# TensorE keeps the planned order in the attention, its first operands load beside the mLSTM, and a quarter of its branch projection becomes filler

## The chip, the cores and the metric

One core of a Trainium2 chip runs the whole kernel. The metric is the device time of one execution in microseconds (us). The core's engines work side by side, each through its own list of instructions in order: TensorE (PE, matmuls; its weight loads are PEld), VectorE (DVE), ScalarE (ACT), GpSimd (POOL) and SyncE (SP, which issues most of the DMA transfers; ACT issues some). They wait for each other by semaphores.

## What is computed

One step of a hybrid encoder layer on 1024 prompt rows and 8 x 16 sample rows, 1152 columns in all, as the kernel keeps tokens along the free axis:

```python
def merge_out(x, h_m, mz, h_a, az, gm, ga, w_bm, w_ba, w_out):
    u_m = jnp.einsum("btc,cd->btd", h_m * jax.nn.silu(mz), w_bm)
    u_a = jnp.einsum("btc,cd->btd", h_a * jax.nn.silu(az), w_ba)
    mix = jax.nn.sigmoid(gm) * u_m + jax.nn.sigmoid(ga) * u_a
    return x + jnp.einsum("btd,de->bte", mix, w_out)
```

Ahead of it stand a norm, one input projection (`w_in`) whose columns are q, k, v and gates of two branches, the mLSTM branch (4 heads of 128, chunkwise, gives `h_m`) and the attention branch (8 heads of 64, each chunk of 64 rows sees itself and 8 chunks before; samples see a cache; gives `h_a`). All is float32; a matmul of two float32 operands is made of three, on high and low halves: hi x hi, hi x lo, lo x hi.

## The kernel before, in words

All names are those of the code below; Lnnn is a line of it.

Stages, by the trace of before: 0 to 122 us input and first projections; 122 to about 410 products of the input projection (`pX`, `pW`, `pZ`); 410 to about 590 the mLSTM; 590 to 930 the attention; 930 to about 984 the branch projection of the attention (`wba`, 8 feature tiles j of 128 rows); then the output projection (`wout`, 8 tiles e).

A feature tile is `load_nt` (L588: weights from memory, split in halves `wh` on ACT and `wl` on DVE or POOL), then chunks of columns, each 3 matmuls for each of 8 (or 4) blocks of 128 rows into a PSUM tile `pm`, then an evacuation. The 16 merge-gate tiles (`gates`) and the 4 z tiles go in chunks of 288 columns (HC); the matmuls are `h_hi,wh`, `h_lo,wh`, `h_hi,wl` (L126 to L128). `g_evac` (L605) writes tanh into `tg`, which is stored to `tg_sc`, from a tag of two buffers. Eight gate tiles are filler in the mLSTM, the rest and the z tiles in the attention.

The attention runs in `run_line`: 32 tiles, four pairs p of heads times eight i of 128 rows. `attend` makes for each of two heads the scores `pS` (L940, L941), a softmax (maximum with bias on DVE, exp on ACT, reciprocal on DVE, scaling on POOL: `prob`), transposes `pT` in groups of up to five (L842), splits `PT` (ACT and DVE), then `pv` (L974). A pair needs `load_q` (two halves), `load_kv` and `load_bias`. The raw operands come through three `raw` buffers on SP and are split by ACT, DVE and POOL. The tile's result goes through `pvs`, `ot` and the store to `o_sc`, and is read again by `load_ops` (L1112) as operands `h2` of the branch projection.

What sets the order: `run_line` is a planner with a clock of its own, `line.now`. It emits the attention's steps when their planned times have come, two tiles alive at a time, and a filler step otherwise: gate and z chunks (`tile_work`), then the 32 chunks of `um_work` (the mLSTM's branch projection, 12 matmuls each, `tm` evacuation with the gate product, stored to `sm_sc`). Thirty filler steps stand ahead of the first. That is the order of the program; the framework's scheduler then orders every engine's instructions, TensorE's among them, by its own rules.

The branch projection: for each j a buffer `sa` (2 buffers) takes `sm_sc[j]` and `tg_sc[8+j]` by two DMAs of 0.59 MB (L1194, L1195). Three chunks of 384 columns (CH) each: DVE makes (tg + 1) * ps (L1199), POOL adds sm (L1200), ACT and DVE split into `x_hi`, `x_lo`. PSUM has six `pm` buffers here, and the output projection reads `x` of all eight j.

Of the kernel before, what the change touches and what calls it, by code (L numbers as in the profile page):

```python
# [6 lines left out]
F32 = mybir.dt.float32  # L7
# [7 lines left out]
P = 128  # L15
# [17 lines left out]
def emit(tc, a, o, ctx):  # L33
# [35 lines left out]
    sm_sc = dram.tile([8, P, T], F32, name="sm_sc")  # L69
    tg_sc = dram.tile([16, P, T], F32, name="tg_sc")  # L70
# [534 lines left out]
    def g_evac(j):  # L605

        def ev(c, ps):
            t_ = stg.tile([P, HC], F32, tag="th", name="tg")
            act.activation(out=t_, in_=ps, func=AF.Tanh, scale=0.5, bias=bh[:, 20 + j:21 + j])  # L609
            store(tg_sc[j], c, t_)  # L610
        return ev

    def z_evac(p):

        def ev(c, ps):
            z_ = stg.tile([P, HC], F32, tag="zs", name="zs")
            t_ = stg.tile([P, HC], F32, tag="th", name="th")
# [9 lines left out]

    esPS, pp = open_pool("pM", bufs=1, space=PSUM)
    esM1, m1 = open_pool("mlstm1", bufs=2, side="right")
    stg = m1  # L630
# [178 lines left out]
    esWp.close()  # L809
    turns = {t_: [wpA] for t_ in turns}  # L810
    stg = keep("stage", bufs=2, side="left")
# [35 lines left out]
    def parts_of(src, half):  # L847

        raw = spl.tile([P, 512], F32, tag="raw", name="raw", bufs=3)
        for x in range(2):  # L850
            sp.dma_start(raw[64 * x:64 * x + 64, :], src[:, half * 512:half * 512 + 512])
        return raw

    def load_q(p, half):
        for j in range(2):
            raw = parts_of(qk_sc[p][64 * j:64 * j + 64], half)
            Qh[p, j, half] = bp_.tile([P, 512], F32R, tag=f"qh{j}{half}", name="q_hi", bufs=1)
            Ql[p, j, half] = bp_.tile([P, 512], F32R, tag=f"ql{j}{half}", name="q_lo", bufs=1)
            split(Qh[p, j, half], Ql[p, j, half], raw, pool)

    def load_kv(p):

        for half in range(2):
            for j in range(2):
                raw = parts_of(qk_sc[4 + p][64 * j:64 * j + 64], half)
                if not half:
                    Kst[p, j] = bp_.tile([P, TP], F32R, tag=f"K{j}", name="Kst", bufs=2)
                k_ = Kst[p, j][:, half * 512:half * 512 + 512]
                act.activation(out=k_, in_=raw, func=AF.Copy)
                dve.tensor_tensor(out=k_[64:128], in0=raw[64:128], in1=f(k_[64:128]), op=ALU.subtract)  # L870
            if not half:
                Vst[p] = bp_.tile([P, NPT, 2, P], F32R, tag="Vst", name="Vst", bufs=2)
            vr = spl.tile([P, 512], F32, tag="raw", name="vraw", bufs=3)
# [47 lines left out]
    def attend(p, i):  # L921
# [59 lines left out]
        zt = ap_.tile([P, P], F32, tag="zt", name="zt", bufs=4)  # L981
# [22 lines left out]
    def sample(p):  # L1004
# [69 lines left out]
        zt = ap_.tile([P, P], F32, tag="zt", name="zt", bufs=4)  # L1074
# [35 lines left out]
    def load_ops(src, k0, order):  # L1110
        for kk, c in order:
            s = slice(c * HC, (c + 1) * HC)  # L1112
            raw = spl.tile([P, 512], F32, tag="raw", name="oraw", bufs=3)[:, 0:HC]
            sp.dma_start(raw, src[kk][:, s])
            split(*hcols(k0 + kk, c * HC, (c + 1) * HC), raw)

    def um_evac(j):

        def ev(c, ps):
            s = slice(c * HC, (c + 1) * HC)  # L1120
            t_ = stg.tile([P, HC], F32, tag="wqr", name="tm", bufs=4)
# [3 lines left out]
        return ev  # L1125

    def run_line():
# [7 lines left out]
        ums = um_work()  # L1135
        work = {"tiles": tile_work()}
        for _ in range(30):
            next(work["tiles"], None)
        line.now += 12000
        while True:  # L1140
# [26 lines left out]
            if not did and not work and ums is not None:  # L1167
# [4 lines left out]
                did = True  # L1172
            if not did:
                if not live and not samples and not work and ums is None:
# [9 lines left out]
    esH.close()  # L1184

# [5 lines left out]
    for j in range(8):  # L1191
        sa = fp.tile([P, 2 * T], F32, tag="sa", name="sa")
        sm, ta = sa[:, 0:T], sa[:, T:2 * T]
        sp.dma_start(sm, sm_sc[j])  # L1194
        sp.dma_start(ta, tg_sc[8 + j])  # L1195

        def ev_a(c, ps):
            s = slice(c * CH, (c + 1) * CH)
            dve.scalar_tensor_tensor(out=ta[:, s], in0=ta[:, s], scalar=1.0, in1=ps, op0=ALU.add, op1=ALU.mult)  # L1199
            pool.tensor_tensor(out=sm[:, s], in0=sm[:, s], in1=ta[:, s], op=ALU.add)  # L1200
            split(x_hi[:, j, s], x_lo[:, j, s], sm[:, s])

        feature_tile(load_nt(a["wba"][j], 4), lambda k, c: hcols(4 + k, c * CH, (c + 1) * CH), ev_a, 4, pp, "pu")
# [5 lines left out]
    for e in range(8):  # L1209
        def ev(c, ps):  # L1210
            xr = stg.tile([P, CH], F32, tag="wqr", name="xr", bufs=4).rearrange("p (i t) -> p i t", i=3)
# [116 lines left out]
```

## Time and profile before

| | us |
|---|---|
| runs | 1092.45, 1094.26, 1095.02 |
| median | 1094.26 |
| profiled execution, its own time | 1090.15 |
| its span | 1088.4 |
| TensorE busy in it | 1039.2 (95%) |
| VectorE, ScalarE, GpSimd busy | 641.5, 527.3, 409.6 |
| TensorE's mean granted clock | 0.991 of full speed |

The profile is of one execution. A window row gives the busy time of each engine in one stretch and, as "PEclk", the granted clock there (1.00 is 2.4 GHz, 0.50 is 1.2 GHz). A wait row tells on which engine and line an engine waited, and for what. A chain row is one piece of the work that ended last: its start, its length and what it was; a DMA in it is counted from issue to landing. Busy time of matmuls includes a modelled drain, so that a lone matmul shows some 0.3 us.

### The profile page before, as it was taken

Reading aid. Unit: us, or ns where it says so; the run is one execution under the profiler, and the core shown is the slowest. Engines: PE = TensorE matmul, PEld = TensorE weight load, DVE = VectorE, ACT = ScalarE, POOL = GpSimd, SP = SyncE. Lnnn points to the kernel's source line nnn. Section 1 sums busy time; section 2 is a strip of 40 time slices with the busy share of each in tenths; the row PEclk is TensorE's granted clock in tenths of the full one; section 3 lists DMA queues with packets and bytes.
Section 4 is the critical chain, followed back from the end, with each engine's and each line's share of the span. In section 5 each row is a group of like instructions: output and inputs, shape, how many; then the busy total and the mean of one; then the engine's idle time right before and its main releaser. Section 6 shows DMA issues by size and latency. Waiting matters only on the chain.

```text
span 1088.4 us, 22458 instructions
## 1 busy us (share of the span) xinstructions
PE 1039.2 (95%) x8090; PEld 1004.9 (92%) x8090; DVE 641.5 (59%) x1561; ACT 527.3 (48%) x1153; POOL 409.6 (38%) x517
## 2 busy tenths in 40 slices
PE   6999999999998999899999999999998998998998
PEld 6999999999998999898999889889898887998998
DVE  6944337585666546799975465354466657574221
ACT  7632147667577554544333566456565535322110
POOL 1132235344353334543334465355454433452000
PEclk8999999999999999899999999999999999999999
DMA  7554332332322228544547675564666874464332
GB/s 240 147 196 149 120 104 84 105 117 95 119 83 81 66 80 285 199 135 163 158 131 251 201 252 178 174 204 130 197 194 196 259 217 140 150 229 144 131 124 72
DMA packets 142516, 171.36 MB, mean 157 GB/s; under 512 B 27900, under 2 KB 106820, under 8 KB 141892
## 3 DMA queue, kind: packets, MB, share of 16 engines
q1 hardware_dynamic: 134196, 159.96, 46.2%
q10 hardware_dynamic: 8208, 9.97, 2.6%
q8 instruction: 64, 1.05, 0.4%
q14 instruction: 48, 0.39, 0.1%
HBM read 118.73 MB, written 51.13 MB: 156 GB/s over the span
## 4 chain that ended last, share of the span: by engine, by line
PE 61%; DMA 16%; DVE 11%; ACT 4%; issue 4%; POOL 2%; SPq 2%; ACTq 0%; DVEq 0%; POOLq 0%
PE pZ L471 10%; PE pm L127 10%; PE pm L126 10%; PE pm L128 10%; PE pW L471 7%; PE pX L471 7%; DMA raw<-qk_sc 3%; DMA sa<-tg_sc 2%; PE pT L842 2%; PE pv L974 2%; DMA oraw<-o_sc 1%; DMA sm_sc<-tm 1%; DMA oraw<-hm_sc 1%; DVE dx L741 1%; DVE kT L658 1%
## 5 line engine op out<-in xcount | busy, mean ns | idle before, releaser
L126 PE MATMUL pm<-h_hi,wh 128*128 128x288 f32 (+1 forms) x864 | 266.0, 308 | 9.4 <-ACT tg L609 6.6
L127 PE MATMUL pm<-h_lo,wh 128*128 128x288 f32 (+1 forms) x864 | 264.9, 307 | 1.1 <-DMA h_lo<-h_sc 1.1
L128 PE MATMUL pm<-h_hi,wl 128*128 128x288 f32 (+1 forms) x864 | 264.3, 306 | 0.0
L122 ACT ACTIVATE wh<-wr 128x512 fp32r<-128x512 f32 (+1 forms) x172 | 107.3, 628 | 151.9 <-PE pm L127 79.0
L126 PEld LDWEIGHTS pm<-h_hi,wh 128*128 128x128 f32 x864 | 164.9, 191 | 13.8 <-ACT tg L609 7.0
L127 PEld LDWEIGHTS pm<-h_lo,wh 128*128 128x128 f32 x864 | 165.1, 191 | 6.5 <-issue 4.2
L128 PEld LDWEIGHTS pm<-h_hi,wl 128*128 128x128 f32 x864 | 164.9, 191 | 1.7 <-issue 0.8
L123 DVE TENSOR_TENSOR wl<-wr,wh 128x512 fp32r<-128x512 f32 (+1 forms) x112 | 82.7, 742 | 40.7 <-ACT wh L122 37.6
L123 POOL TENSOR_TENSOR wl<-wr,wh 128x512 fp32r<-128x512 f32 x60 | 78.7, 1317 | 64.7 <-ACT wh L122 63.9
L450 POOL TENSOR_TENSOR wr<-wr 128x512 f32<-128x512 f32 x48 | 62.6, 1315 | 82.0 <-DVE wl L123 47.3
L833 POOL TENSOR_SCALAR prob<-prob,mx 128x640 f32<-128x640 f32 (+4 forms) x72 | 51.0, 709 | 88.0 <-DVE mx L832 69.4
L126 PE MATMUL pm<-wh,h_hi 128*128 128x256 f32 (+1 forms) x256 | 72.6, 287 | 2.6 <-DVE G L256 2.5
L831 ACT ACTIVATE prob<-prob,mx 128x640 f32<-128x640 f32 (+4 forms) x72 | 51.0, 708 | 47.4 <-DVE mx L830 45.8
L127 PE MATMUL pm<-wl,h_hi 128*128 128x256 f32 (+1 forms) x256 | 72.5, 286 | 0.0
L128 PE MATMUL pm<-wh,h_lo 128*128 128x256 f32 (+1 forms) x256 | 72.0, 284 | 0.0
L126 PE MATMUL pm<-x_hi,wh 128*128 128x384 f32 x192 | 64.8, 338 | 2.6 <-ACT x_hi L122 2.6
L474 DVE TENSOR_TENSOR ring<-pZ,ring 128x288 f32<-128x288 f32 x72 | 32.7, 455 | 58.5 <-PE pZ L471 52.7
L127 PE MATMUL pm<-x_lo,wh 128*128 128x384 f32 x192 | 64.8, 337 | 0.4 <-DVE x_lo L123 0.4
L128 PE MATMUL pm<-x_hi,wl 128*128 128x384 f32 x192 | 64.8, 337 | 0.0
L471 PE MATMUL pW<-S_hi,wh 128*128 128x288 f32 x192 | 56.8, 296 | 0.8 <-ACT ring L483 0.8
L471 PE MATMUL pZ<-S_hi,wh 128*128 128x288 f32 x192 | 56.7, 295 | 0.8 <-DVE ring L474 0.8
L471 PE MATMUL pX<-h_hi,wh 128*128 128x288 f32 x192 | 56.7, 295 | 0.5 <-ACT ring L481 0.5
(278 smaller groups left out, 2830.1 us busy)
## 6 DMA issues: line engine op xcount, KB each, us to landing
wr<-in_wn SPq DMA_DIRECT2D x88, 256.0 KB, 2.7
raw<-qk_sc SPq DMA_DIRECT2D x64, 128.0 KB, 2.8
kr<-in_Kc SPq DMA_DIRECT2D x16, 512.0 KB, 5.7
vr<-in_Vc SPq DMA_DIRECT2D x16, 512.0 KB, 3.2
xt<-in_x SPq DMA_DIRECT2D x9, 512.0 KB
v_sc<-vt SPq DMA_DIRECT2D x72, 64.0 KB, 1.7
u<-u_sc SPq DMA_DIRECT2D x8, 576.0 KB, 4.5
tg_sc<-tg SPq DMA_DIRECT2D x32, 144.0 KB, 2.1
```

What stands on the lines that cost most here:

```text
L122: act.activation(out=hi, in_=raw, func=AF.Copy)
L123: eng.tensor_tensor(out=lo, in0=raw, in1=f(hi), op=ALU.subtract)
L126: mm(ps, lhs[0], rhs[0], start=first, stop=False)
L127: mm(ps, lhs[0], rhs[1], start=False, stop=False)
L128: mm(ps, lhs[1], rhs[0], start=False, stop=last)
L450: pool.tensor_tensor(out=out[:, 0:512], in0=x[:, 0:512], in1=y[:, 0:512], op=ALU.subtract)
L471: mm(ps, w[l][:, k, :], x[r][:, k, :], start=first and k + l + r == 0, stop=k == KH - 1 and l == 1, skip_group_check=True)
L474: eng.tensor_tensor(out=out, in0=x, in1=y, op=ALU.add)
L831: act.activation(out=pt[:, :nk], in_=pt[:, :nk], func=AF.Exp, bias=mx[:, 1:2], accum_out=mx[:, 2:3])
L833: pool.tensor_scalar(out=pt[:, :nk], in0=pt[:, :nk], scalar1=mx[:, 3:4], scalar2=1.0, op0=ALU.mult, op1=ALU.mult)
L842: pe.transpose(pT[:, (n - n0) * P:(n - n0 + 1) * P], pt[:, n * P:(n + 1) * P], ident)
L974: mm(pv[:, j * 256:(j + 1) * 256], Vst[p][:, i + 1 - nb + n, j, :], st[:, n].rearrange("p a q -> p (a q)"), start=n == 0, stop=n == nb - 1)
```

## The change

Four things, and what follows from them in the pools.

1. `run_line()` stands in `tc.manual_schedule(engines={pe.engine})`: TensorE keeps the program's order in the attention, that is the planner's. The other engines stay with the scheduler. The head start grows from 30 to 64 filler steps and from 12000 to 24000 in `line.now`.
2. Pool `attnQ` is opened before the mLSTM. It holds the raw buffers, the first halves of q, and K and V of the even pairs; those of the odd pairs stay in `attnP`. So the loads of the first pair can be issued in the mLSTM, and on SP they stand among the heads' loads there; the first bias load stands on SP ahead of the cache loads `kr` and `vr` and not behind them. To make room, a weight pool is closed before the mLSTM (half as many `wh` and `wl` there), pool `stage` opens before the mLSTM, the gate tanh gets a tag of its own with five buffers, z one `th`, `zt` three, `tm` three.
3. `ua_work` is a new last filler: chunk 0 (288 of 1152 columns) of all eight `wba` tiles, 12 matmuls each, with sm and tg loaded by chunk, and the sum stored to a new scratch `xm_sc`. It may start once three tiles of each pair are done. Each `wba` weight is loaded once more for it.
4. The branch projection goes over pairs of j, in chunks of 288: chunks 1 and 2 of both, then chunk 3 of both, then the split of chunk 0 of both, which comes from `xm_sc`. An `sa` has three DMAs (864 columns of sm, 864 of tg, 288 of the sum).

```diff
-            t_ = stg.tile([P, HC], F32, tag="th", name="tg")
+            t_ = stg.tile([P, HC], F32, tag="tg", name="tg", bufs=5)
...
+    esWp.close()
+    turns = {t_: [wpA] for t_ in turns}
+    stg = keep("stage", bufs=4, side="left")
+    esQ, bq_ = open_pool("attnQ", bufs=1, side="left")
...
-        raw = spl.tile([P, 512], F32, tag="raw", name="raw", bufs=3)
+        raw = bq_.tile([P, 512], F32, tag="raw", name="raw", bufs=3)
...
-                    Kst[p, j] = bp_.tile([P, TP], F32R, tag=f"K{j}", name="Kst", bufs=2)
+                    Kst[p, j] = (bp_ if p % 2 else bq_).tile([P, TP], F32R, tag=f"K{j}", name="Kst", bufs=1)
...
-            t_ = stg.tile([P, HC], F32, tag="wqr", name="tm", bufs=4)
+            t_ = spl.tile([P, HC], F32, tag="wqr", name="tm", bufs=3)
...
+    def ua_evac(j):
+        def ev(c, ps):
+            s = slice(c * HC, (c + 1) * HC)
+            t_, m_ = (q_.tile([P, HC], F32, tag=q, name=q, bufs=3 if q == "wqr" else 2) for q_, q in ((spl, "wqr"), (stg, "zs")))
+            sp.dma_start(t_, tg_sc[8 + j][:, s])
+            sp.dma_start(m_, sm_sc[j][:, s])
+            dve.scalar_tensor_tensor(out=t_, in0=t_, scalar=1.0, in1=ps, op0=ALU.add, op1=ALU.mult)
+            pool.tensor_tensor(out=m_, in0=m_, in1=t_, op=ALU.add)
+            act.dma_start(xm_sc[j], m_)
+        return ev
+    def ua_work():
+        while any((p, i) not in done for p in range(4) for i in range(3)):
+            yield False
+        load_ops(o_sc, 4, [(kk, 0) for kk in range(4)])
+        for j in range(8):
+            w = load_nt(a["wba"][j], 4, eng=pool)
+            yield from chunk(0, w, lambda k, c: h_rhs(4 + k, c), ua_evac(j), 4)
...
-        for _ in range(30):
+        for _ in range(64):
-        line.now += 12000
+        line.now += 24000
...
-    run_line()
-    load_ops(o_sc, 4, [(kk, c) for kk in range(4) for c in range(4)])
+    with tc.manual_schedule(engines={pe.engine}):
+        run_line()
+    load_ops(o_sc, 4, [(kk, c) for c in range(1, 4) for kk in range(4)])
...
+    for j0 in range(0, 8, 2):
+        sas, ws = [], []
+        for j in (j0, j0 + 1):
+            sa = fp.tile([P, 2 * T], F32, tag="sa", name="sa")
+            sas.append((sa[:, 0:T], sa[:, T:2 * T]))
+            for t_, src in zip(sas[-1], (sm_sc[j], tg_sc[8 + j])):
+                sp.dma_start(t_[:, HC:], src[:, HC:])
+            sp.dma_start(sa[:, 0:HC], xm_sc[j])
+            ws.append(load_nt(a["wba"][j], 4))
...
+        for cs in ((1, 2), (3,)):
+            for j in (j0, j0 + 1):
+                for c in cs:
+                    feature_chunk(c, ws[j % 2], lambda k, c: h_rhs(4 + k, c), ev_a(j), 4, pp, "pu", HC)
+        for j in (j0, j0 + 1):
+            split(x_hi[:, j, 0:HC], x_lo[:, j, 0:HC], sas[j % 2][0][:, 0:HC])
```

TensorE in the middle of the attention (last pair), before: `pm` rows are fillers, `x3` stands for three in a row.

```order
L126 MATMUL pm<-h_hi,wh 128x288
L127 MATMUL pm<-h_lo,wh 128x288
L128 MATMUL pm<-h_hi,wl 128x288
L974 MATMUL pv<-PT,Vst 128x256 x3
L842 MATMUL pT<-ident,prob 128x128 x3
L940 MATMUL pS<-Kst,q_hi 128x320
L941 MATMUL pS<-Kst,q_lo 128x320
L940 MATMUL pS<-Kst,q_hi 128x320
L941 MATMUL pS<-Kst,q_lo 128x320
L974 MATMUL pv<-PT,Vst 128x256 x2
L842 MATMUL pT<-ident,prob 128x128 x2
L126 MATMUL pm<-h_hi,wh 128x288
```
And now, around the same kind of step:

```order
L127 MATMUL pm<-h_hi,wh 128x288
L128 MATMUL pm<-h_lo,wh 128x288
L129 MATMUL pm<-h_hi,wl 128x288
L976 MATMUL pv<-PT,Vst 128x256 x5
L844 MATMUL pT<-ident,prob 128x128 x5
L942 MATMUL pS<-Kst,q_hi 128x320
L943 MATMUL pS<-Kst,q_lo 128x320
L942 MATMUL pS<-Kst,q_hi 128x320
L943 MATMUL pS<-Kst,q_lo 128x320
L127 MATMUL pm<-h_hi,wh 128x288
L128 MATMUL pm<-h_lo,wh 128x288
L129 MATMUL pm<-h_hi,wl 128x288
```
The groups of `pv`, `pT` and `pS` are whole now, with twelve filler matmuls ahead of the `pv` and 36 behind the `pS`; before they were split in twos and threes.

TensorE where the attention ends and the branch projection begins (`pm` of 384 columns), before:

```order
L842 MATMUL pT<-ident,prob 128x128 x3
L974 MATMUL pv<-PT,Vst 128x256 x3
L842 MATMUL pT<-ident,prob 128x128 x2
L974 MATMUL pv<-PT,Vst 128x256 x5
L842 MATMUL pT<-ident,prob 128x128 x3
L974 MATMUL pv<-PT,Vst 128x256 x2
L842 MATMUL pT<-ident,prob 128x128 x5
L974 MATMUL pv<-PT,Vst 128x256 x3
L842 MATMUL pT<-ident,prob 128x128 x2
L974 MATMUL pv<-PT,Vst 128x256 x7
L126 MATMUL pm<-h_hi,wh 128x384
```
And now (the `pm` of 288 columns ahead of the last `pv` are fillers of `ua_work`, those behind it the branch projection):

```order
L127 MATMUL pm<-h_hi,wh 128x288
L128 MATMUL pm<-h_lo,wh 128x288
L129 MATMUL pm<-h_hi,wl 128x288
L976 MATMUL pv<-PT,Vst 128x256 x5
L844 MATMUL pT<-ident,prob 128x128 x5
L127 MATMUL pm<-h_hi,wh 128x288
L128 MATMUL pm<-h_lo,wh 128x288
L129 MATMUL pm<-h_hi,wl 128x288
L844 MATMUL pT<-ident,prob 128x128 x5
L976 MATMUL pv<-PT,Vst 128x256 x10
L127 MATMUL pm<-h_hi,wh 128x288
```
The end had no filler before; now filler stands up to the last two softmaxes, three matmuls lie between their transposes, and the last two groups of `pv` come together.

VectorE in the branch projection, its second and third j before (`sa<-sa,pm` is the product with the gate, `x_lo` the split that frees a buffer, `wl` a weight's low half):

```order
L123 TENSOR_TENSOR x_lo<-sa,x_hi 128x384 x3
L1199 SCALAR_TENSOR_TENSOR sa<-sa,pm 128x384 x3
L123 TENSOR_TENSOR wl<-wr,wh 128x512
L123 TENSOR_TENSOR x_lo<-sa,x_hi 128x384 x2
L1199 SCALAR_TENSOR_TENSOR sa<-sa,pm 128x384
L123 TENSOR_TENSOR x_lo<-sa,x_hi 128x384
L1199 SCALAR_TENSOR_TENSOR sa<-sa,pm 128x384
L123 TENSOR_TENSOR x_lo<-sa,x_hi 128x384
```
And its second pair now:

```order
L1242 SCALAR_TENSOR_TENSOR sa<-sa,pm 128x288 x3
L124 TENSOR_TENSOR wl<-wr,wh 128x512
L124 TENSOR_TENSOR x_lo<-sa,x_hi 128x288 x2
L124 TENSOR_TENSOR wl<-wr,wh 128x512
L124 TENSOR_TENSOR x_lo<-sa,x_hi 128x288
L1242 SCALAR_TENSOR_TENSOR sa<-sa,pm 128x288 x3
L124 TENSOR_TENSOR x_lo<-sa,x_hi 128x288 x5
```
Before, products and splits of one j follow each other; now three products of one j, its three splits, three of the other, and then five splits, of which the first is the one of chunk 0 of the first j.

## Rows read from the trace of the kernel before

**Rows 1.** TensorE and the others by stage; busy us (instructions), granted clock, DMA share, GB/s

```profile
410.00:590.00 180.00, 170.63 (x1318) 164.81 (x1317) 148.00 (x397) 76.27 (x168) 70.63 (x115) 0.98 0.56 182
590.00:910.00 320.00, 304.03 (x2769) 282.13 (x2769) 175.04 (x517) 179.19 (x418) 157.42 (x226) 0.99 0.65 202
910.00:930.00 20.00, 15.84 (x110) 13.66 (x110) 14.81 (x42) 11.96 (x28) 9.32 (x15) 1.00 0.33 99
930.00:984.00 54.00, 53.99 (x309) 53.51 (x308) 34.89 (x51) 16.14 (x31) 26.43 (x24) 1.00 0.60 213
984.00:1088.40 104.40, 97.88 (x556) 97.14 (x555) 26.69 (x44) 9.69 (x16) 3.41 (x3) 1.00 0.34 111
```

**Rows 2.** TensorE's waits, whole span; us in total, times, longest us

```profile
PE pm L126 <- ACT tg L609: 6.6, 2, 5.3
PE pS L940 <- DVE mx L828: 5.9, 6, 1.8
...
PE pm L126 <- ACT x_hi L122: 2.6, 1, 2.6
...
PE pT L842 <- POOL prob L833: 2.4, 4, 1.2
```

**Rows 3.** TensorE in three stretches of the mLSTM; busy us (instructions), clock, DMA share, GB/s

```profile
434.00:440.20 6.20, 1.45 (x11) 0.96 1.06 370
440.20:447.00 6.80, 6.29 (x28) 0.54 0.53 186
447.00:460.00 13.00, 13.00 (x107) 1.00 0.56 182
```

**Rows 4.** Chain of waits at 434 to 441; start us, us, what

```profile
434.91 4.48 DMA tg_sc<-tg
...
440.27 0.40 ACT tg L609
```

**Rows 5.** Chain of waits where the attention starts

```profile
590.25 6.30 DMA bias<-in_biasp
596.57 4.38 DMA raw<-qk_sc
```

**Rows 6.** TensorE where the attention starts, by stretch

```profile
590.00:602.00 12.00, 9.34 (x66) 1.00 0.91 296
602.00:610.00 8.00, 7.73 (x47) 0.79 0.95 280
```

**Rows 7.** Chain of waits where the attention ends

```profile
928.11 0.44 PE pT L842 x2
...
929.48 0.50 PE pv L974 x2
```

**Rows 8.** Chain of waits in the branch projection, first load and last load

```profile
935.39 6.46 DMA sa<-tg_sc
...
941.94 0.57 DVE sa L1199
...
979.42 4.72 DMA sa<-tg_sc
...
984.27 0.56 DVE sa L1199
...
987.57 0.45 PE pm L127
```

**Rows 9.** Chain of waits in the products stage: twelve matmuls of 288 columns

```profile
201.25 1.58 PE pW L471 x12
```

**Rows 10.** Groups of instructions by line; busy us, mean ns, then idle time before

```profile
L123 DVE TENSOR_TENSOR h_lo<-oraw,h_hi 128x288 fp32r<-128x288 f32 x30 | 16.6, 561 | 22.0 <-ACT h_hi L122 21.8
...
L1123 DVE SCALAR_TENSOR_TENSOR tm<-tm,pm 128x288 f32<-128x288 f32 x32 | 14.1, 445 | 8.1 <-PE pm L128 4.9 <-DMA tm<-tg_sc 1.4 <-DMA wr<-in_wba 0.8
...
L484 POOL TENSOR_TENSOR ring<-ring 128x288 f32<-128x288 f32 x24 | 22.1, 922 | 88.4 <-ACT ring L483 71.0 <-DMA u_sc<-ring 7.2 <-DMA wr<-in_wn 7.2
...
L123 DVE TENSOR_TENSOR wl<-wr,wh 128x512 fp32r<-128x512 f32 (+1 forms) x112 | 82.7, 742 | 40.7 <-ACT wh L122 37.6
```

More of the change, by code (lines that the diff above doesn't have):

```diff
@@ L69, in emit @@
     sm_sc = dram.tile([8, P, T], F32, name="sm_sc")
+    xm_sc = dram.tile([8, P, HC], F32, name="xm_sc")
     tg_sc = dram.tile([16, P, T], F32, name="tg_sc")
@@ L856, in load_q @@
             raw = parts_of(qk_sc[p][64 * j:64 * j + 64], half)
-            Qh[p, j, half] = bp_.tile([P, 512], F32R, tag=f"qh{j}{half}", name="q_hi", bufs=1)
-            Ql[p, j, half] = bp_.tile([P, 512], F32R, tag=f"ql{j}{half}", name="q_lo", bufs=1)
+            Qh[p, j, half] = (bp_ if half else bq_).tile([P, 512], F32R, tag=f"qh{j}{half}", name="q_hi", bufs=1)
+            Ql[p, j, half] = (bp_ if half else bq_).tile([P, 512], F32R, tag=f"ql{j}{half}", name="q_lo", bufs=1)
             split(Qh[p, j, half], Ql[p, j, half], raw, pool)
@@ L871, in load_kv @@
             if not half:
-                Vst[p] = bp_.tile([P, NPT, 2, P], F32R, tag="Vst", name="Vst", bufs=2)
-            vr = spl.tile([P, 512], F32, tag="raw", name="vraw", bufs=3)
+                Vst[p] = (bp_ if p % 2 else bq_).tile([P, NPT, 2, P], F32R, tag="Vst", name="Vst", bufs=1)
+            vr = bq_.tile([P, 512], F32, tag="raw", name="vraw", bufs=3)
             sp.dma_start(vr.rearrange("p (i d) -> p i d", i=4), v_sc[4 + p][:, 4 * half:4 * half + 4, :])
@@ L1112, in load_ops @@
             s = slice(c * HC, (c + 1) * HC)
-            raw = spl.tile([P, 512], F32, tag="raw", name="oraw", bufs=3)[:, 0:HC]
+            raw = bq_.tile([P, 512], F32, tag="raw", name="oraw", bufs=3)[:, 0:HC]
             sp.dma_start(raw, src[kk][:, s])
@@ L1172, in run_line @@
                 did = True
+            if not did and not work and ums is None and uas is not None:
+                r = next(uas, "end")
+                if r == "end":
+                    uas = None
+                    did = True
+                elif r is not False:
+                    line.now += 400
+                    did = True
             if not did:
-                if not live and not samples and not work and ums is None:
+                if not live and not samples and not work and ums is None and uas is None:
                     break
                 line.now += 100
-    run_line()
-    load_ops(o_sc, 4, [(kk, c) for kk in range(4) for c in range(4)])
+    with tc.manual_schedule(engines={pe.engine}):
+        run_line()
+    load_ops(o_sc, 4, [(kk, c) for c in range(1, 4) for kk in range(4)])
     esPS.close()
@@ L1184, in emit @@
     esH.close()
+    esQ.close()
     esF, fp = open_pool("fin", bufs=2, side="right")
@@ L1190, in emit, with ev_a, ev @@
     x_lo = fp.tile([P, KD, T], F32R, name="x_lo", bufs=1)
[L1191 to L1203, printed above, removed]
+    for j0 in range(0, 8, 2):
[7 more added lines that the diff above has]
+            ws.append(load_nt(a["wba"][j], 4))
+        def ev_a(j):
+            sm, ta = sas[j % 2]
+            def ev(c, ps):
+                s = slice(c * HC, (c + 1) * HC)
+                dve.scalar_tensor_tensor(out=ta[:, s], in0=ta[:, s], scalar=1.0, in1=ps, op0=ALU.add, op1=ALU.mult)
+                pool.tensor_tensor(out=sm[:, s], in0=sm[:, s], in1=ta[:, s], op=ALU.add)
+                split(x_hi[:, j, s], x_lo[:, j, s], sm[:, s])
+            return ev
+        for cs in ((1, 2), (3,)):
[4 more added lines that the diff above has]
+            split(x_hi[:, j, 0:HC], x_lo[:, j, 0:HC], sas[j % 2][0][:, 0:HC])
     def x_rhs(k, c):
```

15 lines of the change are left out of this document (6 added, 9 removed).

## The prediction, made before the changed kernel had run

> **What bounds the kernel now.** I read the stretches by stage first [rows 1]. TensorE is busy 1039 of 1088 us: 304.0 of 320 in the attention, 15.8 of 20 in its last 20 us, 54.0 of 54 in the branch projection, 97.9 of 104.4 in the output projection. So its own work is the bound nearly everywhere, and what a change can take out is its idle time and its low clock. Second, the list of TensorE's waits [rows 2]: the largest is for ACT `tg`, 6.6 us in two waits (one of 5.3), then the softmax (`pS` for DVE `mx`, 5.9 in six waits, `pT` for `prob`, 2.4 in four), then x_hi, 2.6. Third, the chain of waits around each.
>
> All sums are against the profiled execution's own 1090.15 us. That run is the fastest shown, 4.1 below the median of 1094.26, so I carry the difference over to the median. About 0.2% (2.2 us) is what a measurement of this kernel can tell from no change.
>
> **TensorE's work.** Removed and added matmuls nearly cancel. The branch projection took 3 x 96 matmuls of 384 columns, and now 4 x 96 of 288. Twelve of 288 columns take 1.58 us [rows 9], 0.132 each; 309 of 384 fill 54 us [rows 1], 0.175 each. Before, 288 x 0.175 = 50.4; now 384 x 0.132 = 50.7. A quarter of it, 96 x 0.132 = **+12.7 us**, moves into the attention, and 38.0 are left behind it. It pays only as far as it fills idle time there or lets the output projection start earlier.
>
> **The mLSTM.** The chain shows that ACT `tg` at 440.27 waited for its buffer's store, issued at 434.91 and 4.48 us on its way [rows 4]. From 434 to 440.2 TensorE was busy 1.45 of 6.20 us, and the next 6.8 us ran at a granted 0.54, 1.2 GHz, with 28 instructions (3.7 us at 0.132), so 3.1 lost; after that the clock is 1.00 again [rows 3]. With five `tg` buffers in place of two, the sixth tile and not the third waits for a store. That is worth 4.7 + 3.1 = **-7.8 us**, if nothing else is late there. Against it: VectorE is busy 148 of 180 us in this stage [rows 1] and now also gets the first pair's K splits, and the pair's loads stand on SP among the heads' u, V and M rows, with three `raw` buffers, so that a late split holds up what a head waits for. Ends: -7.8 to 0; I take -7.8, since the wait had one cause and the rest of the stage waits little (of rows 2 only this wait lies here), and keep the other end as a rival.
>
> **The attention's start.** The chain runs over the bias load, 590.25 and 6.30 us long, and a raw load of 4.38 [rows 5]; on SP the bias stood behind two cache loads of 0.5 MB each, and now stands ahead of them, with no raw load of the first pair left there. TensorE lost 2.7 us to 602 and ran at 0.79 for the next 8 [rows 6], 1.7 more. The second `pS` now comes 9 fillers after the first, not 48, so a late bias would be felt sooner. Ends -4.4 to +2; I take **-3.0**, nearer to the rows' own loss.
>
> **The attention's middle.** Idle there: 320 - 304.0 = 16.0, less 2.9 at the start, 13 us [rows 1, 6], in waits of about 1 us, most of them for the softmax [rows 2]. The new order sets whole groups: four `pS`, twelve fillers, five `pv`, five `pT`, the next `pS`, then 36 fillers. Between the two `pS` groups lie 12 x 0.132 + 10 x 0.11 (an estimate: 256 columns at the same rate) = 2.7 us; after the 36 fillers there is ample time. Before, the groups were split in twos and threes among odd numbers of fillers. It can cost up to as much as it saves: -13 to +12. I take **-6**, half the idle time, since the long stretches become free of waits and the short ones are no longer than before. Three `tm` buffers in place of four, and two of `m_`, in bursts of one chunk per 1.6 us: +0.5 (0 to 4).
>
> **What it adds beside TensorE.** Eight weight loads of 0.25 MB, 24 transfers of 0.15 MB, and for each of the eight chunks a weight split (POOL), a product of 0.445 (VectorE) and a sum of 0.92 (POOL) [rows 10]. VectorE is busy 175 of 320 us there, POOL 157, and the queues 0.65 [rows 1], so I cost them at nothing; without that cover they would be 8 x 0.445 = 3.6 and 7.4 us. Four buffers of zt that become three, and the later head start of the fillers, I cost at nothing too: the transfers are small and TensorE's work is the same.
>
> **The attention's end.** Before, the last softmaxes have no filler left: 4.2 us idle [rows 1]; and short groups such as the two `pT` of 0.44 us at 928.11 [rows 7] count as busy while they drain, which I put at 2 more. Now chunk 0 of the branch projection fills it: **-6.2**. Two softmaxes remain at the end with three fillers between them, then ten `pv`: the last `prob` and `PT` splits come late, and the next stage's third chunk needs the last tile's `o_sc` store and load. I put this at **+4** (2 to 6), nearest to the old tail's 4.2.
>
> **The branch projection.** Here the loads decide, not TensorE. Before, an `sa` load of 6.46 us at 935.39 held VectorE until 941.94; near the end the load issued at 979.42 lands after 4.72, the product starts at 984.27, and the output projection goes on only at 987.57 [rows 8]: 57.6 us after the last `pv` (929.98). Two `sa` buffers stay two, but they now come in pairs: as the order shows, VectorE makes three products of one j, its splits, three products of the other j, and then the chunk-0 split that frees the first buffer. From landing to that split I count 6 products x 0.445, 4 splits x 0.56, two wl x 0.74 [rows 10] = 6.4 us, about 6.6 with gaps. Then 0.4 of issue and a load of 5 (4.72 to 6.46, for 7/8 of the bytes): **12.0 us a pair**, against 72 x 0.132 = 9.5 on TensorE. First landing 12.0 after the last `pv` (941.94 less 929.98), three cycles of 12.0, and 6.6 plus four more splits of 0.56 for the last pair: 56.8. So the last x is there about as late as before (-0.8), although TensorE has 12 us less to do; it stands idle instead, some 2.5 in each cycle and about 6 ahead of the output projection, where the chunk that its first columns need is split last of all. An idle stretch of 4.7 us ahead of 440.2 was followed by 1.2 GHz [rows 3]; I add 2.5 for that, between 1.7 and 3.1 (rows 6 and 3). Term: **+1.7**, -8 to +8.
>
> The Trainium skill, "TensorE: Matmul & The Clock Gate", section "HAM oscillation — how this bites in real kernels", speaks against this stage: TensorE that waits for a load between batches falls back to 1.2 GHz at each wait and pays it each time. Rows 3 agree on one such wait. By it the three cycles would pay too, up to 3.1 each less the 2.5 of slack, some 2 in all, and the sum would be near -2 instead of -4.
>
> **The sum.** 12.7 - 7.8 - 3.0 - 6 + 0.5 - 6.2 + 4 + 1.7 = **-4.1 us** (the 38.0 us left of the branch projection lie within the 56.8): 1086.1 in the profiled run's terms, 1090.2 in the median's; I say 1090.
>
> **The rivals.**
> - *The freed TensorE time is gained (0.20).* If an `sa` pair comes back within TensorE's 9.5 us (load under 3 us, or splits that free the first buffer early), three cycles save 7.5 and the low clock's 2.5 go: 1080. For it: 7/8 of the bytes, in more pieces. Against: no `sa` load in rows 8 took under 4.7 us.
> - *The fixed order waits (0.16).* TensorE can no longer run a filler ahead of a softmax that is late. Place: the 16 short gaps of 2.7 us between `pS` groups. It decides once VectorE or ACT takes over 2.7 us to empty a `pS`, as where `um` products or sample jobs queue ahead of it. Price: a third of the 16 at 1.0 us (5.9 over 6 waits, rows 2), 5.3, and the 6 don't come: 1090.2 + 11.3 = 1101.5, slower.
> - *The pairs cycle slower (0.13).* If both loads of a pair share the queues, as at 935.39 (6.46), a cycle is 14 us: three times 2 more, 1096. For it: six loads are issued together in the first pair. Against: the second buffer is freed some 2 us after the first.
> - *The mLSTM gives nothing (0.11).* VectorE's chain or SP's order takes the place of the store wait, the 7.8 don't come: 1098.
>
> **How the numbers follow.** Forecast 0.40 (1086 to 1095: faster 0.31, same 0.07, slower 0.02); freed time 0.20, all faster; fixed order 0.16, all slower; slow pairs 0.13 (same 0.03, slower 0.10); mLSTM 0.11 (same 0.02, slower 0.09). Faster 0.51, same 0.12, slower 0.37. Both signs hold much, so the range takes in the rivals on both sides, with some of each one's spread: 1076 to 1104; the forecast's own is 1086 to 1095.
>
> **What would show it.** In the new profile: no wait for ACT `tg` over 1 us and clock 1.00 through the mLSTM (-7.8); the first `pS` pair not held by a bias load (-3); idle time per `pS`, `pT`, `pv` in the middle under 8 us (-6); the last 20 us of the attention nearly filled; `sa` loads 12 us apart per pair, TensorE idle 2 to 3 us in each and about 6 ahead of the output projection, which starts some 57 us after the last `pv`. Wrong if that distance is under 52 (freed time) or over 60 (slow pairs), if the middle has more idle time than 13 us (order), or if the mLSTM is as long as before.

## The result: slower by 1.2%

The changed kernel takes 1103.83 us in the median (1102.46 to 1109.64) where the kernel before takes 1093.36 in the same comparison. The comparison gives a ratio of 1.0116, interval 1.0088 to 1.0144 (the two medians alone give 1.0096). I had forecast 1090, faster; the time lies just inside the upper edge of the range, 1104, but on the other side of no change.

The profile after, TensorE and the others by stage (busy us with instructions for PE, PEld, DVE, ACT, POOL; granted clock; DMA share; GB/s), cut by the changed kernel's own stages (1002 lies some 4 us into the output projection, as 984 does in [rows 1]):

```profile
410.00:600.00 190.00, 181.41 (x1401) 175.03 (x1400) 159.48 (x401) 86.89 (x189) 85.75 (x121) 0.99 0.62 190
600.00:929.00 329.00, 306.82 (x2801) 289.37 (x2800) 172.11 (x528) 176.46 (x410) 158.45 (x233) 0.97 0.63 193
929.00:949.40 20.40, 13.72 (x92) 13.02 (x92) 13.54 (x31) 9.78 (x22) 12.37 (x17) 0.85 0.76 229
949.40:1002.00 52.60, 44.76 (x312) 42.56 (x311) 34.98 (x61) 19.51 (x43) 22.12 (x25) 0.99 0.69 224
1002.00:1103.30 101.30, 97.58 (x556) 96.94 (x554) 26.36 (x46) 8.95 (x16) 2.77 (x3) 1.00 0.36 114
```

Against [rows 1]: the attention is 349.1 us long from the first `pS` (600.2) to the last `pv` (949.3) where it was 337.5 (592.2 to 929.7), its clock falls to 0.97 and, in the last 20 us, to 0.85, and there TensorE is busy 13.7 of 20.4 us. The branch projection and what follows (949.4 to the end) are shorter, 154 us and not 158.

TensorE's waits after, whole span (us in total, times, longest):

```profile
PE pT L844 <- POOL prob L835: 12.1, 5, 5.5
PE pm L127 <- DVE sa L1242: 6.7, 4, 2.7
...
PE pv L976 <- DVE PT L124: 3.9, 5, 2.3
PE pm L127 <- DVE tm L1125: 3.6, 2, 2.2
PE pv L976 <- DVE mx L832: 3.3, 3, 2.0
```

The wait for ACT `tg` of [rows 2] is gone. `pT` now waits 12.1 us for `prob` where it waited 2.4.

For the accounts below each matmul is counted from its start to the next one's start. The median of its form in before is its work; what is over is waiting, or, where the granted clock was 1.2 GHz, low clock. Profiled runs, us:

| stretch | before: work, wait, low clock | after | change |
|---|---|---|---|
| 407 to the first `pS` | 163.5, 19.0, 2.6 | 173.1, 18.2, 1.3 | +9.6 work, -2.1 |
| first 20 us of the attention | 15.5, 2.9, 1.5 | 15.7, 4.3, 0.0 | -0.1 |
| its middle | 253.8, 42.2, 1.5 | 259.0, 43.6, 6.4 | +5.2 work, +6.3 |
| its last 20 us | 13.4, 6.6, 0.0 | 11.3, 7.6, 1.4 | -2.1 work, +2.4 |
| last `pv` to the last matmul | 154.8 long | 150.1 long | -4.7 |

Work ahead of the last `pv` grew by 12.7, as counted (the rows, each rounded, give 12.9). With 0.5 us before 407 the changes sum to 12.7 - 2.1 - 0.1 + 6.3 + 2.4 - 4.7 + 0.5 = 15.0, the difference between the two profiled runs' last matmuls (1099.4 and 1084.5). The medians lie only 10.5 apart; to which stretch the other 4.5 belong is not known. (The wait column has a floor: in the middle of before it has 42.2 us, where TensorE is idle for some 13 [rows 1, 6]. Only differences are used.)

### The profile page after: what moved, and what is told of

It reads as the page before. It is cut to its first block, busy times and chain, and to the rows that moved or that the text cites. A ratio compares the mean times of both kernels' runs of the same rounds, so it can differ in the third digit from the quotient of the medians.

```text
span 1103.3 us, 22777 instructions
## 1 busy us (share of the span) xinstructions
PE 1040.5 (94%) x8186; PEld 1010.0 (92%) x8186; DVE 648.7 (59%) x1577; ACT 533.3 (48%) x1169; POOL 420.7 (38%) x533
## 5 line engine op out<-in xcount | busy, mean ns | idle before, releaser
L127 PE MATMUL pm<-h_hi,wh 128*128 128x288 f32 x896 | 274.0, 306 | 10.6 <-DVE sa L1242 4.8
L128 PE MATMUL pm<-h_lo,wh 128*128 128x288 f32 x896 | 269.3, 301 | 1.2 <-DMA h_lo<-h_sc 1.0
L129 PE MATMUL pm<-h_hi,wl 128*128 128x288 f32 x896 | 268.1, 299 | 0.0
L127 PEld LDWEIGHTS pm<-h_hi,wh 128*128 128x128 f32 x896 | 171.6, 192 | 20.0 <-issue 7.7
L123 ACT ACTIVATE wh<-wr 128x512 fp32r<-128x512 f32 (+1 forms) x180 | 112.6, 629 | 153.9 <-PE pm L128 72.8
L128 PEld LDWEIGHTS pm<-h_lo,wh 128*128 128x128 f32 x896 | 171.4, 191 | 3.1 <-DMA h_lo<-h_sc 1.3
L129 PEld LDWEIGHTS pm<-h_hi,wl 128*128 128x128 f32 x896 | 171.1, 191 | 0.4
L124 POOL TENSOR_TENSOR wl<-wr,wh 128x512 fp32r<-128x512 f32 x68 | 90.5, 1335 | 89.4 <-ACT wh L123 88.7
L124 DVE TENSOR_TENSOR PT<-pT,PT 128x384 fp32r<-128x384 f32 (+3 forms) x96 | 45.0, 483 | 28.2 <-ACT PT L123 27.7
L472 PE MATMUL pW<-S_hi,wh 128*128 128x288 f32 x192 | 56.8, 296 | 0.8 <-ACT ring L484 0.8
```

Source lines behind the costliest of these rows:

```text
L123: act.activation(out=hi, in_=raw, func=AF.Copy)
L124: eng.tensor_tensor(out=lo, in0=raw, in1=f(hi), op=ALU.subtract)
L127: mm(ps, lhs[0], rhs[0], start=first, stop=False)
L128: mm(ps, lhs[0], rhs[1], start=False, stop=False)
L129: mm(ps, lhs[1], rhs[0], start=False, stop=last)
L472: mm(ps, w[l][:, k, :], x[r][:, k, :], start=first and k + l + r == 0, stop=k == KH - 1 and l == 1, skip_group_check=True)
```

## Experiments

Ratios are to the kernel before, in comparisons of their own, with 95% intervals. "Waits" of a stretch are waiting and low clock together, by the account above; before has 54.7 us in the attention, the changed kernel 63.2.

### TensorE's order

```diff
-    with tc.manual_schedule(engines={pe.engine}):
-        run_line()
+    run_line()
```

> The changed kernel with one line undone: TensorE's order in the attention is the scheduler's again; pools, head start, new filler and branch projection in pairs stay. Theory A (the fixed order costs: pT, pv and pS wait in line where the scheduler would have put fillers): the 7.7 us of extra waiting and low clock that the attention shows go, 1103.8 becomes 1094 to 1097. Theory B (the new filler and its transfers load VectorE, ScalarE and the queues, whoever sets the order): 1101 to 1105.

Measured 1.0033 (1.0013 to 1.0052), 1095.8 us. The attention's waits fall from 63.2 to 54.9, before's own level, 5.1 of the 8.3 us in its middle. The fixed order costs some 0.8% and is the larger part of the loss. Alone, on the kernel before:

> The kernel before with TensorE held to the planner's order in the attention, and nothing else changed. Theory A: the attention gets waits as in the changed kernel, 7 to 10 us more than before: 1100 to 1104. Theory B (order is harmless, the rest of the change costs): 1091 to 1096.

Measured 1.0060 (1.0038 to 1.0081), 1098.1 us: slower by itself, by a little less than theory A had. The profiled run's attention has 57.1 us of waits, and 10.9 of them (4.5 in before) lie in its first 20 us, where the first `pS` waits 6.1 us for the first K. The rest of its attention waits no more than before's (46.2 against 50.2), so that on the kernel before the fixed order is seen to cost only there (this profiled run, 1095.7 us, is among its fastest).

### What the fixed order waits for

In the changed kernel's timeline, ACT, VectorE, POOL and TensorE around one wait (start, duration, engine, line, instruction, then idle time and what ended it):

```profile
772.79 0.63 ACT L871 ACTIVATE Kst<-raw 128x512 fp32r<-128x512 f32 x1 [4.11 <-DMA raw<-qk_sc]
773.32 0.48 ACT L610 ACTIVATE tg<-pm,bh 128x288 f32<-128x288 f32 x1
773.70 0.39 ACT L833 ACTIVATE prob<-prob,mx 128x128 f32<-128x128 f32 x1
...
769.57 0.15 DVE L832 TENSOR_SCALAR mx<-mx 128x1 f32<-128x1 f32 x1
...
774.55 0.37 POOL L835 TENSOR_SCALAR prob<-prob,mx 128x128 f32<-128x128 f32 x1 [6.29 <-DVE mx L834]
...
771.49 1.06 PE L1033 MATMUL pS<-kr,QB 128*32 128x512 f32 x8
774.97 0.33 PE L844 MATMUL pT<-ident,prob 128*128 128x128 f32 x1 [2.42 <-POOL prob L835]
```

ACT stood 4.11 us at a split of the next pair's K whose raw load was on its way. Behind it in ACT's order was the exp of a softmax; VectorE had produced its maximum by 769.72. TensorE's next instruction was that softmax's `pT`. So I took the K loads of pairs 1 to 3 away (24 transfers; those pairs' scores are then of another K, while all splits and matmuls stay):

```diff
-                raw = parts_of(qk_sc[4 + p][64 * j:64 * j + 64], half)
+                raw = parts_of(qk_sc[4 + p][64 * j:64 * j + 64], half) if p == 0 else f(Kst[p - 1, j][:, half * 512:half * 512 + 512])
```

> The changed kernel in which pairs 1 to 3 read, for K, the K tile of the pair before, which lies in SBUF, and not the raw tile from memory: the 24 K loads of those pairs are left out (and their heads' scores are of another K), their splits on ACT and VectorE stay. Theory D: in the fixed order TensorE waits for softmaxes that stand on ACT and VectorE behind a K split whose load is on its way (ACT Kst waited 4.1 us for a raw load at 772, the prob behind it and TensorE's pT with it). Then the waits of 2 to 3 us in the middle (635, 690, 770) go, with their low clock: 1094 to 1098. Theory A alone (the planned distances are too short for a softmax as such): 1101 to 1105.

> The control: the kernel before with the edit of the K-resident run (pairs 1 to 3 read K from the tile of the pair before, their 24 K loads left out, the splits stay). If it is the fixed order that makes the K loads dear, the scheduler's order hides them and little is gained: 1088 to 1092. If the loads cost the same under either order, 1079 to 1083 (12 less, as in the changed kernel).

> The fourth corner of a square: the changed kernel with the scheduler's order on TensorE and with K of pairs 1 to 3 read from the tile of the pair before (24 loads left out). So far, against before: changed 1.0116, changed with K resident 1.0005, changed with the scheduler's order 1.0033. If the fixed order costs only through the K loads' waits: the same as the fixed order with K resident, 0.998 to 1.002. If it costs by itself too and the K loads cost 0.7% under any order, as in before: 0.994 to 0.997.

| ratio (waits in the attention, us) | K loaded | K resident |
|---|---|---|
| kernel before | 1 (54.7) | 0.9932, 0.9902 to 0.9963 (49.0) |
| changed, scheduler's order | 1.0033 (54.9) | 0.9981, 0.9957 to 1.0006 (48.4) |
| changed, fixed order | 1.0116 (63.2) | 1.0005, 0.9977 to 1.0034 (48.7) |

With K resident the two orders wait alike, 48.7 and 48.4 us, and their ratios differ by 0.0024, within their intervals. With K loaded they differ by 8.3 us and 0.0083. So most of what the fixed order costs, 0.0059 of 0.0083, it costs through the K loads; in the profiled runs' middle it adds 5.1 us of waits with the loads and none without. (The intervals of the two ratios with K resident leave room for a rest of some 0.006.) I had expected before to gain either nothing or as much; it gains 0.7%, so the loads are no free work there either, and the scheduler's order only softens them.

These runs take the loads' traffic away, K's turns in the three `raw` buffers, and the wait. To tell wait from traffic I kept the loads and moved the splits: all eight raw tiles of a pair are asked for in threes and split one tile later. (The function `ask`, which issues one load and returns its split, is not shown.)

```diff
-        if i == 3 and p < 3:
-            load_q(p + 1, 0)
-            load_kv(p + 1)
+        if 3 <= i < 7 and p < 3:
+            for u in ups.pop((p, i), ()):
+                u()
+            if i < 6:
+                ups[p, i + 1] = [ask(p + 1, k) for k in range(3 * i - 9, min(3 * i - 6, 8))]
```

> The changed kernel, all of its work kept, with the next pair's eight raw tiles asked for in threes at i = 3, 4 and 5 and each three split one tile of the attention later, so that the loads have landed when ACT and VectorE come to the splits. Theory D (in-order splits behind their loads hold up the softmaxes): as the K-resident run, 1091 to 1096. If it was the loads' traffic or the number of transfers and not the wait, 1101 to 1105.

> The kernel before with the same spreading of the next pair's loads and splits. Theory D with a scheduler that hides most of the wait: 1088 to 1092. If before pays as much for its K splits' waits: 1080 to 1086.

Measured 1.0075 (1.0048 to 1.0101) and 0.998 (0.9955 to 1.0006): inconclusive. The first, 1101.6 us, lies in the range that I had given to the traffic, but the edit did not remove the wait: ACT still waited 22.6 us for raw loads in the attention (24.4 without the edit), since the scheduler had put the splits close behind their loads again. (That profiled attention is 7.9 us shorter than the changed kernel's all the same, the stretches around it 4.8 longer: how long ACT waits does not tell what TensorE pays for it.) So the next runs also hold each split behind the exp (ACT) and the reciprocal (VectorE) of the tile in whose step it stands (`made` keeps these two instructions; its two lines are not shown):

```diff
             for u in ups.pop((p, i), ()):
-                u()
+                with tc.issue_after(made["exp"].ins), tc.issue_after(made["rec"].ins):
+                    u()
```

> The changed kernel with the same edit (loads in threes, splits a tile later and behind the exp and the reciprocal). If the fixed order costs through the K loads' waits, most of the step from 1.0116 to 1.0005 comes without leaving the loads out: 1.001 to 1.004. If it is the loads themselves: 1.007 to 1.012, as the spreading alone (1.0075).

> The kernel before, all of its work kept: the next pair's eight raw tiles asked for in threes at i = 3, 4, 5, and each three split one tile later, with the splits held behind that tile's exp on ACT and its reciprocal on VectorE, so that on both engines a softmax no longer stands behind a split whose load is on its way. If the waits for the K loads are what the K-resident run took away (0.9932): 0.993 to 0.996. If it was the 24 loads themselves, their traffic and issue on SP: 0.998 to 1.001, as the spreading alone (0.998).

The changed kernel became far slower, 1.0446 (1.0404 to 1.0488), and yet one stretch of its trace speaks to the question. What VectorE and ACT waited for at the K tiles in the attention (us, times), changed kernel:

```profile
  ACT Kst L871: 27.7, 12
  DMA raw<-qk_sc: 24.4, 12
```

and with the splits held back:

```profile
  ACT Kst L901: 3.5, 7
```

TensorE by stretch (busy us, clock, DMA share, GB/s), changed kernel:

```profile
650.00:700.00 50.00, 49.07 (x448) 1.00 0.59 184
700.00:750.00 50.00, 48.27 (x501) 1.00 0.55 171
750.00:800.00 50.00, 45.25 (x402) 0.96 0.51 158
```

and with the splits held back, with its longest wait behind:

```profile
650.00:700.00 50.00, 50.00 (x526) 1.00 0.62 195
700.00:750.00 50.00, 50.00 (x452) 1.00 0.59 179
750.00:800.00 50.00, 49.74 (x449) 1.00 0.59 181
800.00:850.00 50.00, 24.85 (x191) 0.68 0.41 119
...
PE pm L127 <- ACT h_hi L123: 35.5, 15, 9.7
```

From 650 to 800, at no less traffic, TensorE under the fixed order is idle 0.3 us, against 7.4 in the changed kernel and 4.1 in before. Counted by the same matmuls, from the 25th to the 121st `pS` on `Kst`, the stretch takes 154.1 us (649.5 to 803.6) and not 165.9. So in this stretch it was the wait of ACT and VectorE in their order, not the traffic. (The splits for the last pair, at which 4.8 of the 7.4 us stood, come from 804 on here, behind the stretch.) Then it stands still from 800 on for `h_hi`, the operands of `um_work`: their raw tiles share the three raw buffers, which the late splits hold, and the first of them is split at 819. Whether buffers of their own would keep the first gain without this loss was not tried. On the kernel before, the same edit gives 0.9972 (0.9951 to 0.9992), short of the 0.9932 without the loads. ACT's waits for the K loads fall there from 29.8 to 6.5 us (590 to 950), but TensorE's waits in the profiled attention stay (54.6 against 54.7; this is the slowest of that kernel's twelve runs). So for the scheduler's order wait and traffic are not told apart.

### The head start and the end

The end of the attention in the changed kernel, TensorE:

```profile
940.29 0.29 PE L129 MATMUL pm<-h_hi,wl 128*128 128x288 f32 x1
946.12 1.33 PE L844 MATMUL pT<-ident,prob 128*128 128x128 f32 x5 [5.55 <-POOL prob L835]
947.10 2.59 PE L976 MATMUL pv<-PT,Vst 128*128 128x256 f32 x10
```

and its clock by stretch here and at 635 (busy us, clock):

```profile
940.00:943.20 3.20, 0.58 (x5) 0.99 0.88 278
943.20:950.00 6.80, 3.88 (x18) 0.50 0.58 173
635.00:639.40 4.40, 2.70 (x20) 1.00 0.87 253
639.40:646.20 6.80, 5.88 (x24) 0.50 0.63 192
```

The three matmuls between the last two transposes cover 0.4 of 6 us, and from 943.2, within that wait, TensorE is at 1.2 GHz for 6.8 us, as it is from 639.4, within a wait of 2.3 us. The head start had spent the filler ahead of the attention. Two runs gave some of it back (30 steps and 12000; 54 and 20000):

> The changed kernel with the head start back at 30 filler steps and 12000 of the planner's time: 102 filler matmuls move from ahead of the first pS to the end, where 39 and 15 stand ahead of the last two pT and pv. Theory A: only the wait of 5.7 us ahead of the last pT and its low clock (some 3) go, the waits in the middle stay: 1095 to 1098, unless the first pS, now right behind the mLSTM, waits for its bias (then up to 5 more, 1100 to 1103). Theory C (the early part of the attention is what the head start protects): 1105 or more.

> The changed kernel with a head start of 54 filler steps and 20000: 30 filler matmuls (4 us) move from ahead of the first pS to between the last two pT, where 33 stand in place of 3; fixed order and all else stay. The wait of 5.7 us and its low clock (3 us) at the end should go, the start loses 0 to 3 as the first pS is 4 us nearer to its bias: 1096 to 1101. If the tail wait is not the filler's lack, 1103 to 1106.

Measured 1.0156 (1.0127 to 1.0186) and 1.0122 (1.0091 to 1.0153): no gain. The end did as expected, its last 20 us wait 1.5 and 4.6 where they waited 9.0. But with 30, whose time is theory C's, the first 20 us wait 8.9 (4.3), the stretch up to the first `pS` 5.0 more, and from the last `pv` to the last matmul it takes 163.9 us and not 150.1: 6.8 of filler are still to be done there, and 7 more are waits and low clock. Filler moved to one end is missed at the other. With 54 the stretch up to the first `pS` waits some 2.4 more, the attention 3.1 less; that profiled run is 1.8 us faster than the changed kernel's, the ratios do not differ, and where the medians lose it again is not shown.

### The new filler and the projection in pairs

> The changed kernel without the new last filler, with the branch projection of before (three chunks of 384 per j, two loads); fixed order, early loads and the head start of 64 stay. The attention has 12.7 us less work but, as the order shows, no filler for its last eight softmaxes. Theory A (order, and too little filler at the end): the end waits 8 to 12 us, the projection takes its 155 us again in place of 150: 1103 to 1108. Theory B (the filler's own transfers and evacuations disturb the attention): 1092 to 1097.

Measured 1.0107 (1.0067 to 1.0146), 1102.1 us, just under what theory A had: the end waits 10.7 in its last 20 us, and from the last `pv` on the run takes 155.8. With the fixed order, the filler makes no difference that shows. With the scheduler's order:

> The changed kernel with the scheduler's order and without the new filler and the projection in pairs: pools, early loads and the head start of 64 alone. Against before, pools alone gave 1.0016 and all but the fixed order 1.0033. If the new filler is what costs the rest: 1.000 to 1.002. If it is the head start: 1.003 to 1.005.

Measured 1.0007 (0.9983 to 1.0030), against 1.0033 with the filler. The filler adds 12.7 us of work to the attention; the waits there fall by 1.6 (56.5 to 54.9), and the part behind the last `pv` gets shorter by 8.2 (157.0 to 148.8). That leaves some 3 us to the bad in the profiled runs; the two intervals overlap. The head start by itself costs nothing that shows.

### The pools, in the mLSTM

> The kernel before with two things: five buffers for the gate tanh in the mLSTM, and the weight pool closed ahead of the mLSTM to make room for them. No early loads. By the store-wait theory (the buffer wait was 4.7 and its low clock 3.1): the wait for ACT tg goes and first pS moves 5 to 8 us ahead for the same matmuls, 1085 to 1088. By the rival (the head's own chain on VectorE is as late, the wait only changes its name): other waits grow by as much, 1090 to 1094.

> Of the change only the pools: the first pair's operands load beside the mLSTM, five gate buffers, a weight pool closed early; order by the scheduler, head start 30, no new filler, branch projection of before. If the early loads and the five buffers are worth their 2 us in the mLSTM and the start: 1088 to 1091 where before is 1092. If VectorE's queue in the mLSTM takes it back, as the new waits for mB, mS, mD and mA in the changed kernel say: 1091 to 1097.

> The changed kernel without its early loads: the even pairs' q, K and V and the raw tiles lie in the pool that opens behind the mLSTM, the odd pairs' in the early one, so the first pair can only load once the mLSTM's tiles are free; five gate buffers, fixed order and the rest stay. If the early K splits hold up the heads' chain in the mLSTM (five-buffer run: 12.3 us waiting there, changed kernel: 18.2 and 1.3 at low clock), the mLSTM waits 12 to 14 and the attention's start waits some 4 to 6 more: total 1100 to 1104, no gain or little. If the early loads cost nothing in the mLSTM: 1106 to 1110.

The edit of the first, in the mLSTM alone (the weight pool closed earlier to make room is not shown):

```diff
-            t_ = stg.tile([P, HC], F32, tag="th", name="tg")
+            t_ = stg.tile([P, HC], F32, name="tg", **({"tag": "tg", "bufs": 5} if stg is m1 else {"tag": "th"}))
```

Measured 0.9988 (0.9964 to 1.0011), 1.0016 (0.9991 to 1.0041) and 1.0127 (1.0073 to 1.0181). With five buffers and no early loads, the waits up to the first `pS` are 12.3 us (before 21.6): the full 9 us, and TensorE's clock is 1.00. The kernel is not faster, for the scheduler then runs 96 more filler matmuls ahead of the first `pS`, and the attention's first 20 us wait 16.3 (4.5 before). TensorE in it, mLSTM and what follows (busy us of PE, PEld, DVE, ACT, POOL; clock):

```profile
410.00:595.80 185.80, 181.55 (x1424) 176.22 (x1424) 154.83 (x399) 84.48 (x183) 80.48 (x120) 1.00 0.60 187
595.80:610.00 14.20, 7.10 (x32) 4.93 (x31) 8.31 (x31) 6.93 (x18) 9.59 (x15) 0.75 0.75 219
```

With the early loads in place the waits up to the first `pS` are 18.3 (pools alone) and 19.5 (changed). In the changed kernel's mLSTM TensorE waits for the heads' chain instead:

```profile
PE mB L756 <- DVE C L716: 1.9, 1, 1.9
PE mD L712 <- issue: 1.7, 1, 1.7
PE mS L745 <- DVE dx L749: 1.3, 2, 1.2
PE mA L763 <- DVE num L773: 1.0, 1, 1.0
```

Taking the early loads out of the changed kernel brings these waits to 15.2, and the attention then has 69.5 (63.2), so the total is no better (1.0127 against 1.0116). The early loads cost about 4 us in the mLSTM and save about as much at the start.

### Candidates

> A candidate: the kernel before with five gate buffers in the mLSTM (alone 0.9988) and the next pair's operand loads spread over three tiles (alone 0.998). If the two add up: 0.996 to 0.998. If the 9 us that the mLSTM saves go into an attention that lacks its filler, as in the five-buffer run, 0.998 to 1.001.

> A candidate: the pools of the change alone (first pair's operands beside the mLSTM, five gate buffers; 1.0016 before) with the edit of the two runs above. If the pin is worth what the K-resident run gave and the early loads cost nothing more: 0.993 to 0.997. Else 0.999 to 1.002.

Measured 1.0014 (0.9987 to 1.0040) and 1.0007 (0.9986 to 1.0028): neither adds up. Of the versions that do all the work, the only one clear of the kernel before is that kernel with its K splits held behind the softmax, 0.9972 (0.9951 to 0.9992), 1090.4 us, and narrowly.

## Why the prediction was wrong, step by step

- **TensorE's work: right.** 12.7 us moved ahead of the last `pv`.
- **The middle of the attention: the step that failed.** I gave the fixed order -6, "half the idle time", from the distances in TensorE's own list. The middle came out 6.3 longer in the profiled run: 1.4 of waiting and 4.9 of low clock; 5.1 of it are gone under the scheduler's order. What I had wrong is that a planned distance of 2.7 us, as long as before, is enough: the distance a softmax needs isn't its own length; it is that plus whatever stands ahead of it on ACT and VectorE. My rival named the place right (no filler can run ahead of a late softmax), and its price for the waits, 5.3, is near the 6.3, but it put the cause in `um` products and sample jobs; that it came so close is in part luck. The main cause is the next pair's K splits, which wait for loads (at 799 it is a split of V, for which ACT stood 2.55 us). The row that told it was in the trace of before, ACT's waits from 600 to 950:

```profile
ACT Kst L869 <- DMA raw<-qk_sc: 28.3, 14, 3.2
```

  VectorE waits after it. I read TensorE's waits and not theirs. Without the first pair's, before has 25.4 us in 12 waits and the changed kernel 24.4 in 12: ACT waits alike, and the order of TensorE decides what that costs.
- **`tm`: +0.5 forecast, more measured.** TensorE waits 3.6 us for `tm` in the changed kernel's attention and 1.8 in before, and the wait of 2.2 us at 875 is one of those with low clock (3.4 us) behind it. VectorE stood 4.75 us there for a load of `tm`, which SP had issued only after a wait of 5.3 us for the store that frees one of the three buffers. With four buffers and the fixed order alone the waits for `tm` are 4.9 us, so that how much of it the third buffer's loss makes is not shown.
- **The mLSTM: right cause, wrong sum.** The store wait was worth what I said (9 us in the five-buffer run, forecast 7.8). In the changed kernel 2.1 came. ACT stands 6.0 us there, in three waits, at the early K splits (449 to 466), and TensorE's longest wait of the stage, 1.9 us for `mB` until 457.9, lies among them; without the early loads 4.3 of the missing 7.2 come back, and the rest is not located. That was my fourth rival, at 0.11.
- **The attention's start: -3 forecast, -0.1 measured** in its first 20 us; the 8 us ahead of the first `pS` wait 1.0 less, which the account has with the mLSTM.
- **Its end: -6.2 + 4 forecast, +2.4 measured.** The filler stops one softmax short, as the order showed. The wait is 5.55 and not 4, and I left out the low clock behind it.
- **The branch projection: +1.7 forecast, -4.7 measured.** The loads came as I read them; the overlap behind them did not. SP's loads of one buffer and the chain's landing times (start us, us), then the output projection's first matmul and, in the chain, its first on the last x:

```profile
957.06 0.38 SPq L1233 DMA_DIRECT2D sa<-sm_sc  x1
...
969.31 0.33 SPq L1233 DMA_DIRECT2D sa<-sm_sc  x1
...
981.50 0.33 SPq L1233 DMA_DIRECT2D sa<-sm_sc  x1
...
993.03 0.33 SPq L1233 DMA_DIRECT2D sa<-sm_sc  x1
...
981.88 3.89 DMA sa<-tg_sc
...
993.40 4.09 DMA sa<-tg_sc
...
998.22 0.41 PE L127 MATMUL pm<-x_hi,wh 128*128 128x384 f32 x1 [1.94 <-DVE sa L1242]
...
1006.14 0.44 PE pm L128
```

  The cycle is 12.25, 12.2 and 11.5 us (forecast 12.0), the load 3.9 to 4.1 (forecast 5), and the chain goes on at 1006.14, 56.4 us after the last `pv` (949.69; forecast 56.8, before 57.6). But TensorE does not stand idle for 6 us until then. It begins the output projection at 998.22 on x that is split already, and 43 of its matmuls run ahead of 1006.14, where 22 ran ahead of 987.57 in before: 21 x 0.175 = 3.7 us that I had not counted. And the 2.5 for low clock never came: TensorE waits 6.7 us in four pieces for `sa`, 2.7 at most, and the clock stays 0.99. The Trainium skill, "TensorE: Matmul & The Clock Gate", section "HAM oscillation — how this bites in real kernels", has the clock fall at each wait where the work of a batch is shorter than the wait for its next load. The trace agrees for the wait of 5.55 us at 946, for `prob` and not for a load, with three matmuls ahead of it (0.50 from 943.2 on); the four waits here stand between batches of some 9.5 us of work, so that I had drawn on the page for a case that it does not describe.

The sum forecast was -4.1; 15.0 came. Of the 19.1 between them the middle is 11.8 (forecast -6 and +0.5 for `tm`, measured +6.3 together), mLSTM and start 8.6 (-10.8, -2.2), the end 4.6 (-2.2, +2.4), the projection -6.4, and 0.5 came ahead of 407, where nothing was changed.

## What to carry to other kernels

Before an engine's order is fixed, look at what the other engines wait for in theirs: a split that waits for a load on ACT holds up every softmax behind it, and a scheduler that may move TensorE's instructions softens that. Order such consumers behind the urgent work, and look first at what else needs their loads' buffers (buffers of their own were not tried here). Filler pays only where it stands at a wait: moved earlier to cover one end it leaves the other bare. Work that moves out of a load-bound stage doesn't shorten the loads' chain (57.6 and 56.4 us here); it gains where the next stage can begin beside it.

## What I had not expected of the hardware

By the account above the clock made somewhat more of the attention's loss than the waits. In five places of the changed kernel's attention (639, 776, 800, 875 and 943 us) a wait of 2.2 to 5.6 us came with 3.4 or 6.8 us at 1.2 GHz, from within it or right behind it; before had two such stretches (604 and 877), behind waits of 1.0 and 1.8. Of the 8.5 us that the attention lost, 4.7 were low clock. The length of a wait doesn't tell which: the one of 2.7 us in the branch projection had none behind it, nor had one of 2.5 at 606.
